# Six pairs of projection units by seven half products in a hybrid encoder layer

## The chip, the core and the metric

The kernel runs on one core of one Trainium2 chip. The core has five engines with a queue of instructions each: PE (TensorE, matmuls and the loads of their weights), DVE (VectorE), ACT (ScalarE), POOL (GpSimd) and SP, which here only issues DMA transfers. The metric is the device time of one execution in microseconds (us), lower is better.

## The reference, cut to what matters

One encoder layer on 512 tokens of width 1024: projections of `x`, partial rotary embedding, two attention mixers, sigmoid gates, an output projection, layer norm, a SwiGLU feed-forward part and a second layer norm.

```python
proj = h @ w_in[l]
qa, ka, va, qb, kb, vb = jnp.split(proj, SPLITS, axis=-1)
qa = rope_partial(qa.reshape(b, s, A_Q_HEADS, HEAD_DIM), pos)      
...
o_a = windowed_gqa_sink(qa, ka, va, a_sink[l])
o_b = dilated_mixture(qb, kb, vb)
gates = jax.nn.sigmoid(h @ w_gate[l] + b_gate[l])
g_a, g_b = jnp.split(gates, N_BRANCH, axis=-1)
mixed = g_a * (o_a @ w_br_a[l]) + g_b * (o_b @ w_br_b[l])
h = layer_norm(DN_ALPHA * h + mixed @ w_out[l], ln1_g[l], ln1_b[l])
f = (jax.nn.silu(h @ w_ff_gate[l]) * (h @ w_ff_up[l])) @ w_ff_down[l]
h = layer_norm(DN_ALPHA * h + f, ln2_g[l], ln2_b[l])
```

## The kernel before

Everything is float32 in and out, and matmuls run in fp32r. A float32 operand is therefore split into a high part (rounded to fp32r) and a low part (the rest), and each product is three matmuls: high times high, high times low, low times high. Making the two parts of a 128x512 tile is a copy (on ACT, or on DVE) and a subtraction on DVE.

Weights come in *units* of 128 output features by 1024 inputs. A unit is loaded as two halves of 128x512 (256 KB), each split by `half_unit` (line 389) into `h` and `l`. `feat_x` multiplies a unit with all of `x`: eight steps over the inputs, three matmuls of 512 columns each, 24 in all, into one PSUM bank. `xh` and `xl` are the two parts of `x`, features on the partitions and tokens along the columns.

What follows a unit depends on its kind. A query or key unit is rotated (`rotate`, line 514: a multiplication by cosines, a shuffle of partitions, a multiplication by sines and a sum, four DVE instructions on 128x512, although only 16 rows of each head's 64 rotate), split into parts, and moved by small DMAs into the layout that the scores want (`q_post`, `k_post`, `k_pairs`). A gate unit goes through a tanh (`gate`, line 1001) and waits in SBUF. A value unit is turned by transposes.

The string `ORDER` (line 79) lists the steps in program order: `q2` is a query unit of mixer A, `k1` a key unit, `g` a gate, `VA` the values, `A0` to `A3` the attention of mixer A by groups of heads, `Q`, `K`, `V` and `B` the same for mixer B. Behind it come the two branch products (L496 to L498 again), the output projection with the first layer norm (`tok_major`, L1192 to L1194) and the feed-forward part. There, pairs of gate and up units are already multiplied by *seven half products* (`quad` and its class, L1422 to L1424): a 2x2 block product of Winograd's form, whose factors are sums of quarter blocks and whose matmuls have 256 columns.

Order on the engines is set by `Program`: the code registers operations with their reads, writes and a priority, and a list scheduler in the kernel then emits them engine by engine, with planned durations and limits on buffers (`ws` staged weight halves, `whl` weight parts, `gen` other tiles). Weights have priority -130 us against the running sum of PE time, so they are fetched as early as their buffers allow: six staged halves and twelve parts while the projections run. Every engine then runs its list strictly in order. `load_sum` (line 367) loads one block and lets a DMA that accumulates, issued by POOL, add a second block to it; the feed-forward part uses it.

```python
def split(src, h, l, prio=0.0, abs_prio=None, hold=()):
    op(cp_alts(S), lambda e: copy(e, h.t, src.t), ...)                       # ACT or DVE
    op([(DVE, dve(S))], lambda e: nc.vector.tensor_tensor(l.t, src.t, f32(h.t), op=ALU.subtract), ...)
```

## Time and profile before

| | us |
|---|---|
| median of 3 runs | 737.44 (737.26 to 737.69) |
| the profiled execution, its own time | 737.0 |
| its span, first to last instruction | 735.2 |
| PE busy in the span | 725.2 |
| DVE busy | 653.7 |
| ACT busy | 447.4 |
| POOL busy | 109.5 |

The span is shorter than the execution's time by what lies around the program. A row of the profile's groups reads: line, engine, operation, tiles written <- tiles read (`ps` a PSUM bank, `sl` an SBUF tile, `x` the parts of `x`), shapes, count | busy time in us, mean ns of one | idle time of that engine just ahead of them and what ended it. Matmuls overlap, so the busy time of a group can be shorter than its count times its mean. A row of the timeline reads: start, length, engine, line, operation, tiles, count [idle ahead of it and what ended that]. A row of the windows gives the stretch, its length, and the busy time and count of PE, PEld (the loads of weights), DVE, ACT and POOL, the granted clock, the DMA engines' share and GB/s.

### The profile page before, as it was taken

What the parts mean: (1) busy time and instruction counts of PE and PEld (TensorE: products, weight loads), DVE (VectorE), ACT (ScalarE), POOL (GpSimd) and SP (SyncE); (2) the same over time, 40 slices, a digit from 0 to 9 for tenths busy, and PEclk for the clock granted to TensorE, in tenths of its full rate; (3) what the DMA queues carried; (4) which work ended last, traced back from release to release, by engine and by line L of the source; (5) the groups of instructions that cost most, each with busy time, mean ns of one, the idle gap of its engine ahead of it and who ended that gap; (6) DMA issues with size and microseconds to landing.
All of it is one profiled execution on the core that took longest, in us unless ns stands there. A gap on an engine that the chain in (4) does not pass through costs nothing.

```text
span 735.2 us, 13431 instructions
## 1 busy us (share of the span) xinstructions
PE 725.2 (99%) x4479; PEld 663.0 (90%) x4479; DVE 653.7 (89%) x1428; ACT 447.4 (61%) x1012; POOL 109.5 (15%) x273
## 2 busy tenths in 40 slices
PE   9999999999999999999999999999999999999995
PEld 6888888888888889888888999999999999999985
DVE  5879998898898999897686999799999999899977
ACT  5647687757665657774352567656666556666721
POOL 0000110000003323500010002111102111202100
PEclk9999999999999999999999999999999999999999
DMA  8824523437234765455583389776888978978402
GB/s 270 289 58 144 163 82 87 129 94 204 76 93 138 201 176 163 137 170 174 165 205 88 86 250 233 178 179 154 203 254 195 221 196 237 243 196 180 112 29 86
DMA packets 69252, 120.17 MB, mean 163 GB/s; under 512 B 8576, under 2 KB 12800, under 8 KB 69184
## 3 DMA queue, kind: packets, MB, share of 16 engines
q1 hardware_dynamic: 59040, 101.10, 44.7%
q0 software_dynamic: 9872, 18.09, 15.2%
q8 instruction: 35, 0.57, 0.3%
q14 instruction: 33, 0.27, 0.1%
q10 hardware_dynamic: 272, 0.13, 0.1%
HBM read 103.04 MB, written 2.10 MB: 143 GB/s over the span
## 4 chain that ended last, share of the span: by engine, by line
PE 94%; DMA 2%; DVE 2%; SPq 1%; ACT 1%; issue 0%; DVEq 0%; ACTq 0%
PE ps L497 12%; PE ps L496 12%; PE ps L498 12%; PE ps L1422 9%; PE ps L1424 9%; PE ps L1423 9%; PE ps L1633 4%; PE ps L1635 4%; PE ps L1634 4%; PE ps L749 3%; PE ps L1192 3%; PE ps L1193 3%; PE ps L1194 3%; PE ps L647 1%; PE ps L646 1%; PE ps L815 1%
## 5 line engine op out<-in xcount | busy, mean ns | idle before, releaser
L357 ACT ACTIVATE sl<-sl 128x512 fp32r<-128x512 f32 (+3 forms) x383 | 210.6, 582 | 62.0 <-DVE sl L1312 17.3
L1312 DVE TENSOR_TENSOR sl<-sl,sl 128x512 fp32r<-128x512 f32 (+3 forms) x294 | 167.1, 609 | 6.2 <-ACT sl L357 3.4
L357 ACT ACTIVATE sl<-ps 128x256 f32<-128x256 f32 (+5 forms) x205 | 85.8, 441 | 99.7 <-PE ps L1424 60.1
L496 PE MATMUL ps<-x,sl 128*128 128x512 f32 (+1 forms) x369 | 142.4, 386 | 0.3 <-ACT x L357 0.3
L498 PE MATMUL ps<-x,sl 128*128 128x512 f32 (+1 forms) x369 | 139.8, 379 | 0.0
L497 PE MATMUL ps<-x,sl 128*128 128x512 f32 (+1 forms) x337 | 127.9, 379 | 0.2 <-DVE x L469 0.2
L1422 PE MATMUL ps<-sl,sl 128*128 128x256 f32 x352 | 96.9, 275 | 0.6 <-ACT sl L357 0.6
L1423 PE MATMUL ps<-sl,sl 128*128 128x256 f32 x352 | 96.8, 275 | 0.0
L1424 PE MATMUL ps<-sl,sl 128*128 128x256 f32 x352 | 96.8, 275 | 0.0
L383 DVE TENSOR_TENSOR sl<-sl,sl 128x512 fp32r<-128x512 f32 x130 | 87.2, 685 | 5.1 <-ACT sl L357 4.5
L498 PEld LDWEIGHTS ps<-x,sl 128*128 128x128 f32 x369 | 69.9, 189 | 9.9 <-DVE sl L406 0.2
L496 PEld LDWEIGHTS ps<-x,sl 128*128 128x128 f32 x369 | 70.2, 190 | 8.7 <-ACT x L357 0.5
L371 POOL DMA_DIRECT2D sl<-wpack x44 | 38.5, 883 | 260.3 <-DMA sl<-wpack 72.7
L1422 PE MATMUL ps<-x,sl 128*128 128x256 f32 x264 | 72.6, 275 | 0.0
L1423 PE MATMUL ps<-x,sl 128*128 128x256 f32 x264 | 72.6, 275 | 0.0
L1424 PE MATMUL ps<-x,sl 128*128 128x256 f32 x264 | 72.6, 275 | 0.0
L497 PEld LDWEIGHTS ps<-x,sl 128*128 128x128 f32 x337 | 64.0, 190 | 7.5 <-DVE x L469 0.5
L1422 PEld LDWEIGHTS ps<-sl,sl 128*128 128x128 f32 x352 | 67.6, 192 | 0.8 <-ACT sl L357 0.7
L1423 PEld LDWEIGHTS ps<-sl,sl 128*128 128x128 f32 x352 | 67.6, 192 | 0.1
L1424 PEld LDWEIGHTS ps<-sl,sl 128*128 128x128 f32 x352 | 67.6, 192 | 0.0
L1422 PEld LDWEIGHTS ps<-x,sl 128*128 128x128 f32 x264 | 50.6, 192 | 0.4
L1423 PEld LDWEIGHTS ps<-x,sl 128*128 128x128 f32 x264 | 50.6, 192 | 0.4
(151 smaller groups left out, 1547.1 us busy)
## 6 DMA issues: line engine op xcount, KB each, us to landing
sl<-wpack SPq DMA_DIRECT2D x243, 256.0 KB, 3.7
sl<-sl SPq DMA_DIRECT2D x108, 128.0 KB, 2.3
wf<-wpack SPq DMA_DIRECT2D x51, 256.0 KB, 5.0
sl<-wpack POOLq DMA_DIRECT2D x44, 256.0 KB, 5.9
wf<-wpack POOLq DMA_DIRECT2D x24, 256.0 KB, 6.3
sl<-xtok SPq DMA_DIRECT2D x8, 256.0 KB, 3.3
out<-sl SPq DMA_DIRECT2D x7, 256.0 KB, 2.0
sl<-xT SPq DMA_DIRECT2D x6, 256.0 KB, 5.6
```

The lines of the kernel that those rows point to most:

```text
L357: nc.scalar.activation(dst, src, AF.Copy)
L371: op([(POOL, 1.0)], lambda e: nc.gpsimd.dma_start(b.t, src2, accum_op=ALU.add), reads=[b], writes=[b], prio=prio, moves=1.65)
L383: op([(DVE, dve(S))], lambda e: nc.vector.tensor_tensor(l.t, src.t, f32(h.t), op=ALU.subtract), reads=[src, h], writes=[l], prio=prio, abs ...
L496: mm(o, a, x0, start=(k == 0 and begins), stop=False, skip_group_check=split)
L497: mm(o, a, x1, start=False, stop=False, skip_group_check=split)
L498: mm(o, b, x0, start=False, stop=(k == nk - 1), skip_group_check=split)
L1312: op([(DVE, dve(w))], lambda e: nc.vector.tensor_tensor(dst(), x(), y(), op=o), reads=reads, writes=writes, prio=prio)
L1422: mm(o, wh, pairs(bh[k]()), start=(first and k == 0), stop=False, skip_group_check=True)
L1423: mm(o, wh, pairs(bl[k]()), start=False, stop=False, skip_group_check=True)
L1424: mm(o, wl, pairs(bh[k]()), start=False, stop=(k == 3), skip_group_check=True)
L1633: mm(ps.t, x0, pairs(w[0].t), start=(first and m == 0), stop=False, skip_group_check=True)
L1634: mm(ps.t, x0, pairs(w[1].t), start=False, stop=False, skip_group_check=True)
```

## The change

**Six pairs.** Twelve units of the first half of `ORDER` (q2 to q7, k1 and five gates) are taken in pairs `P:a,b` by `pair_x`, with the same seven half products as in the feed-forward part. A pair needs seven weight factors of 128x512 instead of four halves; two of them are sums made by an accumulating DMA, two are sums made on DVE, and all seven are split, the high part on ACT and the low part on DVE. Each of the seven products is 12 matmuls of 256 columns. Of `x`, three of the seven products take blocks as they are and four take combinations; `x_forms` makes the combinations once, in place in the tiles in which `x` was loaded, and splits them (16 DVE instructions on 128x256, 8 copies on ACT, 8 subtractions on DVE).

**Rotation.** At `R`, `turn_rows` gathers the 16 rotating rows of each head from two to four tiles into one tile by small DMAs, rotates that tile by the four DVE instructions, and sends the rows back by small DMAs. The tables of cosines and sines come once more in this layout, by 16 DMAs. Units outside the pairs are copied from PSUM on ACT first (`in_sbuf`). Nineteen units rotate so, in six steps `R`; the first three (k0, q0, q1) rotate as before.

**Low parts by DMA.** For the second half of each unit from Q00 to the output projection (two gates aside), `low_by_dma` writes `-w`, rounded, on ACT where the subtraction on DVE stood, and a DMA on POOL's queue adds `w` at full precision; the rounding of the negative copy leaves the same low part.

**Room.** `ws` is 8 and `whl` 16 until the last pair is done (`L`), then 6 and 12 as before; `gen` is 60. Five gates (of 8 to 15) are stored to DRAM behind their tanh and fetched again ahead of the branch products. `ORDER` is rewritten.

```diff
-N_WS, N_WHL, N_ATT = 6, 12, 16
+N_WS, N_WHL, N_ATT, N_GEN = 6, 12, 16, 60
 ORDER = """
-g2 VA q1 A0 q2 q3 A1 g k1 q4 g q5 A2 g q6 g q7 A3 g2
-Q00 K00 Q01 K01 V12 Q02 K02 V0 B0 Q10 K10 B1 Q11 K11 Q12 K12 B2 B3 g8
+X g2 VA q1 A0 P:q2,q3 P:k1,q4 R A1 P:g,g P:q5,g P:q6,q7 R A2 P:g,g A3 g2 L Q00 K00 Q01 K01 R V12 Q02 K02 R V0 B0 Q10 K10 Q11 K11 R B1 Q12 K12 R B2 B3 g7
 """
+BY_DMA = {*range(U_QKB, U_DOWN)} - {U_GATE + 8, U_GATE + 9}
+AWAY = range(8, 16)
+N_WSA, N_WHLA = 8, 16
...
     def half_unit(u, j):
         st, h, l = slot(F32, "ws"), slot(F32R, "whl"), slot(F32R, "whl")
         load(st, wpack[u, :, j * S:(j + 1) * S], prio=-LOOK)
+        if j == 1 and u in BY_DMA:
+            low_by_dma(st, h, l, wpack[u, :, j * S:(j + 1) * S], -LOOK)
+            return h, l
         split(st, h, l, prio=-LOOK, hold=[(l, "room")])
         return h, l
+    def low_by_dma(st, h, l, src, prio):
+        op(cp_alts(S), lambda e: copy(e, h.t, st.t), reads=[st], writes=[h, (l, "room")], prio=prio)
+        op([(ACT, act(S))], lambda e: nc.scalar.activation(l.t, st.t, AF.Copy, scale=-1.0), reads=[st], writes=[l], prio=prio)
+        op([(POOL, 1.0)], lambda e: nc.gpsimd.dma_start(l.t, src.bitcast(F32R), accum_op=ALU.add), reads=[l],
+           writes=[l], prio=prio, moves=1.65)
...
+    def x_forms():
...
+            tt(x11, x11, x12, ALU.subtract, a, a, HP, FORMS)
+            tt(x12, x22, x12, ALU.subtract, a + b, a, HP, FORMS)
+            minus_sum(x22, x11, x22)
+            minus_sum(x21, x22, x21)
+            for kk, toks in ((k, a), (k + 4, b)):
+                h, l = slot(F32R), slot(F32R)
+                parts((lambda h=h: h.t, h), (lambda l=l: l.t, l, (l, "room")), lambda b=xs[kk]: b.t, toks, S, FORMS)
+                XP[kk] = (h, l)
...
+    def pair_x(ua, ub):
...
+        for key in ("A11", "S1", "A12", "S3", "A22"):
+            fetch(key)
+        sep("A11")
+        sep("A12")
+        form("S2", "A11", "S1", "A11")
+        sep("S2")
+        sep("S1")
+        form("S4", "A12", "A12", "S2")
+        for key in ("S3", "S4", "A22"):
+            sep(key)
+        y, xz, t, v = bank("dense"), bank("dense"), slot(), slot()
+        def product(s, b, ps, tok, c, first, after=()):
...
+                for k in range(4):
+                    wh, wl = h.t[:, k * P:(k + 1) * P], l.t[:, k * P:(k + 1) * P]
+                    mm(o, wh, pairs(bh[k]()), start=(first and k == 0), stop=False, skip_group_check=True)
+                    mm(o, wh, pairs(bl[k]()), start=False, stop=False, skip_group_check=True)
+                    mm(o, wl, pairs(bh[k]()), start=False, stop=(k == 3), skip_group_check=True)
...
+        product("A11", "B11", y, "y", LO, True)
+        keep(t, LO, 1, y, "y", LO)
+        product("A12", "B21", xz, "x", LO, True)
+        product("S2", "T2", y, "y", LO, False)
+        keep(t, HI, 2, y, "y", LO)
+        product("S1", "T1", xz, "z", HI, True)
+        keep(v, HI, 2, xz, "z", HI)
+        product("S3", "T3", y, "y", LO, False)
+        product("S4", "B22", xz, "z", HI, False)
...
+        product("A22", "T4", y, "y", LO, False)
+        keep(v, LO, 1, y, "y", LO, -1.0)
...
+    def turn_rows(tiles):
...
+        for i, R in enumerate(tiles):
+            for h in range(2):
+                gs.append((G, 2 * i + h))
+                op([(SP, 0.1)], lambda e, R=R, i=i, h=h: nc.sync.dma_start(
+                    G.t[32 * i + 16 * h:32 * i + 16 * h + 16], R.t[64 * h:64 * h + 16]), reads=[(R, 1), (R, 2)], writes=[gs[-1]], prio=EV)
...
+    def put_away(f):
+        t, d = gz[f], Buf("dram", None, lambda: dram.tile([P, S], F32, name=name("gz")))
+        op([(SP, 0.73)], lambda e: nc.sync.dma_start(d.t, t.t), reads=[t], writes=[d], prio=EV)
```

Three places show how instructions stand now. The names are a tile and its number; `x` and `sl` are SBUF tiles.

On PE, early in mixer A, ahead of the first transposes of its probabilities. Before, the three matmuls of a step of unit q3, between them and the next step two matmuls of the scores (L646, L647):

```order
L496 MATMUL ps_610<-x_94,sl_443 128x512
L497 MATMUL ps_610<-x_103,sl_443 128x512
L498 MATMUL ps_610<-x_94,sl_444 128x512
L646 MATMUL ps_637<-sl_351,sl_599 128x256
L647 MATMUL ps_637<-sl_352,sl_599 128x256
L646 MATMUL ps_643<-sl_351,sl_599 128x384
```

Now, at the same row numbers, a product of the second pair with `x` as it is (`ps_705`), and behind it one of the first pair (`ps_620`), whose moving tiles are combinations of `x`:

```order
L627 MATMUL ps_705<-x_94,sl_610 128x256
L628 MATMUL ps_705<-x_103,sl_610 128x256
L629 MATMUL ps_705<-x_94,sl_611 128x256
L627 MATMUL ps_620<-sl_205,sl_506 128x256
L628 MATMUL ps_620<-sl_206,sl_506 128x256
L629 MATMUL ps_620<-sl_205,sl_507 128x256
```

Matmuls of 256 columns stand where matmuls of 512 stood, and products of two pairs alternate.

On DVE, while `x` arrives: before, only low parts of `x` (L469) and of the first weights (L406).

```order
L469 TENSOR_TENSOR x_103<-sl_131,x_94 128x512
L406 TENSOR_TENSOR sl_184<-sl_138,sl_183 128x512
L469 TENSOR_TENSOR x_204<-sl_147,x_192 128x512
L406 TENSOR_TENSOR sl_202<-sl_151,sl_201 128x512
L406 TENSOR_TENSOR sl_211<-sl_157,sl_210 128x512
L469 TENSOR_TENSOR x_204<-sl_164,x_192 128x512
L469 TENSOR_TENSOR x_204<-sl_168,x_192 128x512
L469 TENSOR_TENSOR x_204<-sl_175,x_192 128x512
```

Now the combinations (L532 with 256 columns, L558) and their low parts (L532 with 512) stand between them:

```order
L532 TENSOR_TENSOR sl_98<-sl_98 128x256
L484 TENSOR_TENSOR x_103<-sl_131,x_94 128x512
L532 TENSOR_TENSOR sl_73<-sl_147,sl_73 128x256
L420 TENSOR_TENSOR sl_187<-sl_138,sl_186 128x512
L484 TENSOR_TENSOR x_211<-sl_147,x_195 128x512
L532 TENSOR_TENSOR sl_206<-sl_73,sl_205 128x512
L420 TENSOR_TENSOR sl_215<-sl_152,sl_214 128x512
L420 TENSOR_TENSOR sl_223<-sl_159,sl_222 128x512
L484 TENSOR_TENSOR x_211<-sl_166,x_195 128x512
L484 TENSOR_TENSOR x_211<-sl_170,x_195 128x512
L484 TENSOR_TENSOR x_211<-sl_177,x_195 128x512
L558 SCALAR_TENSOR_TENSOR sl_147<-sl_73,sl_147 128x256
```

The first weights' low parts moved behind one or two of the new rows, and the rest of the combinations follows behind the last part of `x`.

On SP, at the first `R`: before, a query unit's four moves (L587) and then weights (L365).

```order
L587 DMA sl_752<-sl_734 64x512
L587 DMA sl_758<-sl_734 64x512
L587 DMA sl_752<-sl_735 64x512
L587 DMA sl_758<-sl_735 64x512
L365 DMA sl_788<-wpack 128x512
```

Now the gathers (L697) of the third and fourth tile, the weights (L369) between them, and the rows on their way back (L708):

```order
L697 DMA sl_819<-sl_749 16x512 x2
L369 DMA sl_999<-wpack 128x512
L697 DMA sl_819<-sl_915 16x512 x2
L369 DMA sl_1106<-wpack 128x512
L369 DMA sl_1109<-wpack 128x512
L369 DMA sl_1146<-wpack 128x512
L708 DMA sl_659<-sl_819 16x512 x2
L369 DMA sl_1170<-wpack 128x512
L708 DMA sl_724<-sl_819 16x512 x2
L369 DMA sl_1192<-wpack 128x512
L708 DMA sl_749<-sl_819 16x512 x2
L708 DMA sl_915<-sl_819 16x512 x2
```

Loads of weights that stood behind four moves now stand among gathers and returns, each of which can make the loads behind it wait.

More of the change, by code (lines that the diff above doesn't have):

```diff
@@ new lines, in parts, with hl, minus_sum @@
+    def parts(h, l, src, reads, n, prio, whole=True):
+        copy_by_act(h[0], src, n, False, reads, [h[1], l[2]], prio)
+        tt(l[0], src, lambda: f32(h[0]()), ALU.subtract, [*reads, h[1]], [l[1]], n, prio)
+    def hl(st, prio):
+        h, l = slot(F32R, "whl"), slot(F32R, "whl")
+        parts((lambda: h.t, h), (lambda: l.t, l, (l, "room")), lambda: st.t, [st], S, prio)
+        return h, l
+    XP, done_rows = {}, set()
+    def x_forms():
+        at = lambda k, n: (lambda b=xs[k]: b.t[:, n * HP:(n + 1) * HP])
+        key = lambda k: [(xs[k], 0), (xs[k], S // 2)] if k == 0 else [(xs[k], 0)]
+        for k in range(KD // 2):
+            a, b = key(k), key(k + 4)
+            x11, x12, x21, x22 = at(k, 0), at(k, 1), at(k + 4, 0), at(k + 4, 1)
+            def minus_sum(dst, x, y):
+                op([(DVE, dve(HP))], lambda e: nc.vector.scalar_tensor_tensor(
+                    dst(), x(), -1.0, y(), op0=ALU.mult, op1=ALU.subtract), reads=a + b, writes=b, prio=FORMS)
+            tt(x11, x11, x12, ALU.subtract, a, a, HP, FORMS)
[6 more added lines that the diff above has]
+                XP[kk] = (h, l)
@@ new lines, in x_tokens @@
+    def x_tokens(kind):
+        if kind[0] == "B":
+            j, n = int(kind[1]) - 1, int(kind[2]) - 1
+            ks = range(4 * j, 4 * j + 4)
+            mk = lambda m: [lambda k=k: m[k]()[:, n * HP:(n + 1) * HP] for k in ks]
+            return mk(xh), mk(xl), [t for k in ks for t in xtok_of(k)]
+        j, n = {"T1": (0, 0), "T3": (0, 1), "T4": (1, 0), "T2": (1, 1)}[kind]
+        v = [XP[k] for k in range(4 * j, 4 * j + 4)]
+        mk = lambda p: [lambda x=x: x[p].t[:, n * HP:(n + 1) * HP] for x in v]
+        return mk(0), mk(1), [b for x in v for b in x]
@@ L515, in rotate, with in_sbuf @@
+    def in_sbuf(u):
+        ps, t = bank("dense"), slot()
+        feat_x(ps, unit(u))
+        op([(ACT, act(S, True))], lambda e: copy(ACT, halves(t.t), back(ps.t)), reads=[ps], writes=[(t, 1), (t, 2)], prio=EV)
+        return t
     def rotate(ps):
+        if ps in done_rows:
+            return ps
+        if "slot" in ps.keys:
+            return turned(ps)
         R, Sh = slot(), slot()
@@ L671, in evac @@
                         copy(e, d, s)
[L673 removed]
+            op(cp_alts(S, True, 0.3 if turn_by else 0.1)[:2 if turn_by else 1], evac, reads=[ps], writes=[t], prio=EV if i else NORM)
             src.append(t)
```

155 lines of the change are left out of this document (132 added, 23 removed).

## The prediction

> **What bounds the kernel now.** I read the page first, then the windows by stage, then the timelines of PE and DVE. The page:
>
> ```profile
> span 735.2 us, 13431 instructions
> PE 725.2 (99%) x4479; PEld 663.0 (90%) x4479; DVE 653.7 (89%) x1428; ACT 447.4 (61%) x1012; POOL 109.5 (15%) x273
> PE 94%; DMA 2%; DVE 2%; SPq 1%; ACT 1%; issue 0%; DVEq 0%; ACTq 0%
> ```
>
> PE is busy throughout and the chain that ended last is PE's to 94%. A busy PE need not be a PE at its rate, since matmuls overlap. The timeline shows the rate by the distance of starts:
>
> ```profile
> 344.69 0.38 PE L496 MATMUL ps<-x,sl 128*128 128x512 f32 x1
> ...
> 346.63 0.38 PE L496 MATMUL ps<-sl,sl 128*128 128x512 f32 x1
> ...
> 444.77 0.28 PE L1423 MATMUL ps<-sl,sl 128*128 128x256 f32 x1
> ...
> 446.11 0.28 PE L1423 MATMUL ps<-sl,sl 128*128 128x256 f32 x1
> ```
>
> Nine starts lie between the first two rows, so a matmul of 512 columns costs 1.94/9 = 0.216 us; twelve between the other two, so one of 256 columns, in the half products of the feed-forward part, costs 1.34/12 = 0.112. The lengths, 0.38 and 0.28, are latency and must not be added up. By stage:
>
> ```profile
> 0.00:18.50 18.50, 16.81 (x68) 12.25 (x69) 10.86 (x25) 10.27 (x21) 0.90 (x5) 1.00 0.83 270
> 18.50:45.00 26.50, 26.50 (x130) 23.30 (x129) 19.39 (x37) 16.35 (x31) 1.66 (x8) 1.00 0.56 199
> 45.00:61.00 16.00, 16.00 (x80) 14.13 (x79) 15.96 (x41) 8.30 (x23) 2.36 (x7) 1.00 0.49 133
> 61.00:110.00 49.00, 49.00 (x269) 43.93 (x268) 44.81 (x115) 38.09 (x88) 5.05 (x17) 1.00 0.44 124
> 110.00:220.00 110.00, 110.00 (x587) 98.05 (x586) 101.56 (x265) 75.34 (x183) 6.48 (x34) 1.00 0.40 113
> 330.00:400.00 70.00, 69.57 (x324) 60.58 (x323) 50.44 (x82) 28.36 (x49) 6.05 (x7) 1.00 0.62 169
> ```
>
> From 18.5 us on PE never rests in the projections and the attention (26.50 of 26.50 to 110.00 of 110.00), at a granted clock of 1.00. So what the change takes off DVE gains nothing by itself there: only fewer columns through PE, or a wait put into PE, moves the end. But DVE is nearly full as well: 15.96 of 16.00 us from 45 to 61, 44.81 of 49.00 behind that. Its idle time lies at the start: 18.50 - 10.86 = 7.6 us in the first stretch and 26.50 - 19.39 = 7.1 us in the second.
>
> **What is removed from PE.** A pair was two units, 48 matmuls of 512 columns: 48 x 0.216 = 10.35 us. It becomes seven products of 12 matmuls of 256 columns: 84 x 0.112 = 9.38 us. Six pairs save 6 x 0.97 = 5.8 us. The rows of PE confirm it: 216 more in the order, six times 84 - 48, and all other shapes in equal number. That is the whole possible gain: 735.2 - 5.8 = 729.4 us of span.
>
> The Trainium skill speaks against it: its page "TensorE: Matmul & The Clock Gate", section "Back-to-back issue gap", gives 81 ns for a matmul of 128 columns and 131 ns for one of 512 in a sustained stream, because each also pays for its load of weights. An estimate on that page's line, 98 ns for 256 columns, would make a pair 84 x 0.098 - 48 x 0.131 = 1.9 us dearer, and the six 12 us. The spacings above, 0.216 and 0.112, contradict it in this kernel, so it keeps only a small chance below.
>
> **What is added to DVE, and when.** The first place where PE has to wait for DVE is the transposes of mixer A's first probabilities:
>
> ```profile
> 57.28 0.68 DVE L383 TENSOR_TENSOR sl<-sl,sl 128x512 fp32r<-128x512 f32 x1
> 57.88 0.01 DVE L519 LOAD_MASK_SELECT sl<-ps  x1
> 57.88 0.73 DVE L519 STREAM_SHUFFLE sl<-ps 128x512 f32<-128x512 f32 x1
> 58.51 0.16 DVE L805 RECIPROCAL st<-st 128x4 f32<-128x4 f32 x1
> 59.71 0.34 DVE L739 TENSOR_SCALAR sl<-sl,st 128x256 f32<-128x256 f32 x1
> ...
> 441.36 0.42 DVE L1312 TENSOR_TENSOR sl<-sl 128x256 f32<-128x256 f32 x1
> ...
> 442.70 0.68 DVE L1312 TENSOR_TENSOR sl<-sl,sl 128x512 fp32r<-128x512 f32 x1
> 61.05 1.04 PE L749 MATMUL ps<-ident,sl 128*128 128x128 f32 x8
> ```
>
> The row at 59.71 is DVE's last share in these probabilities and the PE row is the transposes, one microsecond later. The distances of starts are DVE's prices: 0.60 us for a 128x512 operation, 0.63 for a shuffle, and 1.34/4 = 0.34 for one on 128x256 (four lie between the two rows of 441 and 442). In the order, DVE has 95 rows up to that normalisation before, and 125 now: 17 more of 128x512 (low parts of seven factors a pair instead of four, sums of factors, parts of the combined `x`), 17 more of 128x256 (the combinations), two shuffles and two copies fewer. That is 17 x 0.60 + 17 x 0.34 - 2 x 0.63 - 0.6 = 14.0 us more ahead of the same point. PE now reaches this point 1.0 us later in its own work (so many columns more of projections stand ahead of it), at 62.0.
>
> DVE was busy 10.86 + 19.39 + 15.96 = 46.2 us up to 61.0. With 14.0 more it needs 60.2, so of the 14.8 us that it idled it may keep 1.8 if PE is not to wait. How much can it fill? These rows show the idle time:
>
> ```profile
> 3.78 0.42 DVE L469 TENSOR_TENSOR x<-sl,x 128x256 fp32r<-128x256 f32 x1 [2.64 <-ACT x L357]
> 8.51 0.69 DVE L469 TENSOR_TENSOR x<-sl,x 128x512 fp32r<-128x512 f32 x1 [1.00 <-ACT x L357]
> 12.02 0.69 DVE L469 TENSOR_TENSOR x<-sl,x 128x512 fp32r<-128x512 f32 x1 [0.77 <-ACT x L357]
> 14.05 1.37 DVE L406 TENSOR_TENSOR sl<-sl,sl 128x512 fp32r<-128x512 f32 x2
> 40.68 0.76 DVE L695 TENSOR_TENSOR sl<-ps,sl 128x256 fp32r<-128x256 f32 x2 [4.07 <-ACT sl L357]
> ```
>
> The 3.5 us before 3.78 stay, since no input has landed. The gaps at 8.51 and 12.02 can take the first three combinations (1.0 us), which the order puts there. The 4.07 us ahead of 40.68 vanish: combinations and weight factors are queued. Left are 3.5 us at the start, 0.6 more before 6 us, and of the 2.6 us in gaps from 8 to 12 us about 1.6: 5.7 us, where 1.8 are free. That makes a wait of 3.9. Against that, operations that waited for ACT one by one were spaced by 1.37/2 = 0.68 (their full length), and in a backlog go at 0.60; for some 30 of the 95 rows that gives back 2.4, a wait of 1.5. Between these ends I take 2.4.
>
> From there to about 110 us the six pairs run. In a pair DVE does 7 low parts, 2 sums of factors, one sum of two blocks (10 x 0.60) and 0.34, 6.3 us in 9.38 us of PE, with mixer A's softmax besides. Before, two query units cost it four low parts, eight operations of rotation and two low parts behind, 14 x 0.60 = 8.4 in 10.35. The rotations shrink from 22 times four operations to 9 times four, but the gate pairs had none. Softmax chains that left DVE 4.2 us idle in 61 to 110 will do so again, with less room; I put 0.6 us of wait there, between nothing and the 1.5 that a full repeat of the first wait's lower end would be. Behind 110 the removed rows leave DVE room, which PE cannot use.
>
> **Rotation in common.** Nineteen tiles each cost two gathers and two returns, 76 small DMAs, and 16 for the tables. The nearest rows:
>
> ```profile
> 54.56 2.39 SPq L587 DMA_DIRECT2D sl<-sl  x4
> sl<-sl SPq DMA_DIRECT2D x108, 128.0 KB, 2.3
> sl<-wpack SPq DMA_DIRECT2D x243, 256.0 KB, 3.7
> sl<-wpack POOLq DMA_DIRECT2D x44, 256.0 KB, 5.9
> ```
>
> At 0.60 us an issue (2.39/4) and 2.3 to land, a step of four tiles takes 8 x 0.60 + 2.3 out, 4 x 0.60 on DVE and 7.1 back, 16.6 us, then 2.6 us of parts and moves. The shortest cover in the order is at Q12 and K12: 125 matmuls, about 24 us of PE, between K12's last matmul and the first score that reads a tile of theirs, and that step has only two tiles (4.7 + 2.4 + 4.7 + 5 us). So it costs nothing; the rest have 30 us and more. What waits behind them on SP are loads of weights, late by a return at most, 7.1 us, against a room of six halves, 6 x 12 x 0.216 = 15.5 us. I take 0; without that cover it would be up to 5 us once.
>
> **Low parts by DMA.** 41 subtractions leave DVE (41 x 0.60 = 25 us, worth nothing on a PE without gaps), 41 copies go to ACT, which has room (75.34 of 110), and 41 loads to POOL's queue. A low part is ready after its load (3.7), two copies (0.62 each), POOL's 0.9 and 5.9 to land: 11.7 us, inside the 15.5. No term; with that cover gone, see the third rival. The accumulating loads cost DMA time:
>
> ```profile
> q1 hardware_dynamic: 59040, 101.10, 44.7%
> q0 software_dynamic: 9872, 18.09, 15.2%
> L371 POOL DMA_DIRECT2D sl<-wpack x44 | 38.5, 883 | 260.3 <-DMA sl<-wpack 72.7 <-DVE sl L1312 65.5 <-DVE sl L1148 51.9
> ```
>
> q1 moves 256 KB (0.262 MB) in 0.447 x 735.2 x 0.262/101.1 = 0.85 us of all engines, q0 in 1.62. Five gates stored and fetched add ten of the former.
>
> **The sum.** Span 735.2 - 5.8 + 2.4 + 0.6 = 732.4. The profiled execution's own time is 737.0, 1.8 above its span, and the median 737.44, 0.44 above that: **734.6 us**.
>
> **Rivals.**
>
> *All hidden* (0.15): DVE's early work fits because loads land sooner or fewer waits bind, and PE never waits. 737.4 - 5.8 = 731.6. For it: PE rests nowhere from 18.5 to 220 us in the windows above, with the same dense DVE. Against it: 14.0 us more DVE work into 14.8 us of idle time, 4.1 of it before 6 us.
>
> *DVE becomes the bound of the first 110 us, and the kernel slower* (0.12). Its queue is in order: if the combinations of `x` stand ahead of rows whose inputs are there already, or themselves wait for late tiles, the gaps are not filled but shifted. If all 14.8 us of idle time stayed, the normalisation would come 14.0 us later, at 59.7 + 14.0 + 0.3 = 74.0 instead of 62.0, a wait of 12.0: 737.4 - 5.8 + 12.0 = 743.6. The point where it decides: slower than before once DVE idles more than 1.8 + 5.8 = 7.6 us ahead of the first transposes.
>
> *The DMA engines* (0.13). From 330 to 400 us they were busy 0.62 x 70 = 43 us. Some 15 accumulating loads belong there now (15 x 1.62 = 24) and five fetched gates (4.3): 72 us of 70. The surplus of 2.3, with loads landing late behind it, would make PE wait about 3 us beside DVE's: 737.6. For it: a landing of 5.9 us as median already. Against it: weights are fetched ahead, and with 0.83 of share in the first 18.5 us transfers still came.
>
> *The change does not do what it says* (0.03): a 256-column matmul costs more than half of a 512 one where moving tiles come from many SBUF tiles. With the lengths instead of the spacings, six times 84 x 0.28 - 48 x 0.38 = 32 us more, 769; the page's estimate above would give 749. The quads of the feed-forward part already run so at 0.112.
>
> **How the numbers follow.** The forecast has 0.57. Its own range is 732.5 to 736.3 (waits of 1 to 4.7). The range of eight in ten reaches down to the case without a wait and up into the DMA rival and the first part of the DVE rival, 731.6 to 738.8. What three runs can tell from no change is about 0.2%, 1.5 us: faster means below 736.0, slower above 738.9. Faster: 0.53 of the forecast, all 0.15 of *all hidden*, 0.02 of the DMA case, 0.70. Same: 0.04 + 0.09 + 0.04 (DVE half filled), 0.17. Slower: 0.08 + 0.02 + 0.03, 0.13.
>
> **What would show it.** PE's windows of 20 us between 45 and 110 should show starts of 256-column matmuls 0.112 apart and rows of PE with idle time ahead, ended by DVE or by ACT behind DVE, of 3 us in sum, most of them between 45 and 65 us. DVE should have no gap of 4 us before its first value parts, and still a few behind 110. The stretch from 110 to the branch products should be without waits on PE, as before. If PE's waits there are longer than 1 us and end on a DMA, rotation or low parts are priced wrongly; if they sit between 330 and 400 and end on weights, the DMA rival holds; if the early waits exceed 5.8 us, DVE was the bound and the kernel is not faster.

## The result and the profile after

The changed kernel is slower: 761.54 us median of six runs (759.33 to 765.28) against 737.72 for the kernel before on the same chip, a ratio of 1.033 (95% interval 1.030 to 1.036). The profiled execution took 763.23 us, its span is 761.5; the span before was 735.2. So 26.3 us came on top where 2.8 were forecast to go.

The page of the changed kernel:

```profile
span 761.5 us, 14271 instructions
PE 730.9 (96%) x4695; PEld 671.7 (88%) x4695; DVE 645.9 (85%) x1419; ACT 481.0 (63%) x1084; POOL 149.7 (20%) x326
PE 82%; DVE 5%; DMA 2%; ACT 2%; issue 1%; SPq 1%; DVEq 0%; ACTq 0%
...
sl<-sl SPq DMA_DIRECT2D x108, 128.0 KB, 3.5
```

The chain that ended last was PE's to 94% and is so to 82%. DVE is busy for 85% of the span where it was for 89%, ACT for 63% where it was for 61%: no engine has become the bound, waits have come in. The same stages as in the prediction, of the changed kernel (length, then busy time of PE, PEld, DVE, ACT and POOL, PE's granted clock, DMA share, GB/s):

```profile
18.50:45.00 26.50, 23.72 (x110) 20.48 (x109) 22.80 (x46) 16.60 (x30) 3.46 (x4) 0.96 0.89 261
45.00:61.00 16.00, 14.98 (x112) 13.99 (x110) 15.97 (x37) 10.92 (x26) 4.56 (x10) 0.96 0.57 105
61.00:110.00 49.00, 44.03 (x369) 43.30 (x370) 42.33 (x92) 34.79 (x83) 7.14 (x14) 0.98 0.78 201
110.00:220.00 110.00, 106.95 (x596) 95.39 (x596) 90.51 (x243) 78.62 (x190) 15.52 (x50) 0.95 0.62 157
220.00:330.00 110.00, 102.32 (x554) 91.28 (x554) 77.82 (x231) 72.91 (x185) 31.21 (x103) 0.97 0.69 166
330.00:400.00 70.00, 70.00 (x361) 62.17 (x360) 54.57 (x126) 47.73 (x105) 28.66 (x74) 1.00 0.95 255
```

PE rested nowhere from 18.5 to 330 us before (from 220 to 330, which the prediction does not show, it was busy for 110.00 of 110.00). Now it rests 2.8, 1.0, 5.0, 3.0 and 7.7 us in the first five of these stages, 19.5 in sum, and in the same stages its clock is under 1.00: 0.04 x 26.5 + 0.04 x 16 + 0.02 x 49 + 0.05 x 110 + 0.03 x 110 = 11.5 us at most, since part of the low clock falls into the waits. With the 5.8 us that PE has less to do, 26.3 + 5.8 = 32.1 us are to be explained; waits and clock are up to 31.0 of them. What PE waited for (us in total, times, longest):

```profile
PE ps L1153 <- DVE sl L983: 7.7, 1, 7.7
PE ps L627 <- ACT sl L635: 4.4, 2, 4.0
PE ps L890 <- ACT sl L361: 2.8, 1, 2.8
PE ps L1024 <- ACT sl L361: 2.3, 1, 2.3
PE ps L855 <- DMA sl<-sl: 1.6, 1, 1.6
```

A few long waits, at 312.7, 108.5, 43.4, 214.5 and 62.0 us. The longest, in the chain of waits of the changed kernel (start, length, what; the issues of L841 are eight):

```profile
300.07 0.34 PE ps L958 x3
300.48 1.18 SPq L841
...
305.17 0.58 SPq L841
305.80 0.59 SPq L697
306.43 1.94 DMA sl<-sl
...
308.48 0.09 DVE sl L700
...
312.23 0.35 DVE sl L983
312.71 1.20 PE ps L1153 x4
```

and on SP and DVE at the same time:

```profile
296.01 3.77 SPq L796 DMA_DIRECT2D sl<-sl  x6
299.88 5.87 SPq L841 DMA_DIRECT2D sl<-sl  x8
305.80 1.23 SPq L697 DMA_DIRECT2D sl<-sl  x2
308.46 0.01 DVE L700 LOAD_MASK_SELECT sl<-sl  x1 [7.98 <-DMA sl<-sl]
```

Read it from the end. PE wants the low part (L983) of a tile of probabilities. PE's transposes for that tile (L958) ended at 300.4, but L983 stands in DVE's queue behind a common rotation's shuffle (L700), which waited 7.98 us for rows. The last two gathers of rows (L697) were issued at 305.8, because moves (L796 and L841) of the *previous* common rotation's tiles stood ahead of them in SP's queue, the fourteen shown at 0.63 to 0.73 us each (3.77/6, 5.87/8) and ten more before them: 24 in all, from 287.5 to 305.75 us. The tile that these gathers read had been copied out of PSUM by 284.1.

At 108.5 and 214.5 it is the same queue with another victim, ScalarE:

```profile
98.61 7.72 SPq L796 DMA_DIRECT2D sl<-sl  x10
106.01 0.63 ACT L361 ACTIVATE sl<-sl 128x512 fp32r<-128x512 f32 x1 [4.35 <-DMA sl<-sl]
203.10 5.04 SPq L841 DMA_DIRECT2D sl<-sl  x8
208.24 4.89 SPq L369 DMA_DIRECT2D sl<-wpack  x8
213.19 0.63 ACT L361 ACTIVATE sl<-sl 128x512 fp32r<-128x512 f32 x1 [5.09 <-DMA sl<-wpack]
```

In the first, ScalarE's copy (L361) waits 4.35 us until one of these ten moves has landed: the move was issued at 100.92 and landed at 105.58, 4.66 us later (the median of all moves is 3.5), at a DMA share of 0.91 in these 20 us. So there the bunch is late by its landing as well as by its issue. In the second there are eight moves, and the weight loads begin at 208.24, so that a copy of weights holds ScalarE for 5.09 us, with what PE needs behind it.

That reading made the theories for the experiments. *SP*: SyncE's queue, filled by the common rotation's gathers, returns and collected moves, is late, and DVE and ACT stand in order. *DMA*: the accumulating loads fill the DMA engines, and transfers land late. *VectorE*: the pairs overload DVE.

### The profile page after: what moved, and what is told of

It is laid out like the page before. It is cut to its first block, busy times and chain, and to the rows that moved or that the text cites. A ratio compares the mean times of both kernels' runs of the same rounds, so it can differ in the third digit from the quotient of the medians.

```text
span 761.5 us, 14271 instructions
## 1 busy us (share of the span) xinstructions
PE 730.9 (96%) x4695; PEld 671.7 (88%) x4695; DVE 645.9 (85%) x1419; ACT 481.0 (63%) x1084; POOL 149.7 (20%) x326
## 4 chain that ended last, share of the span: by engine, by line
PE 82%; DVE 5%; DMA 2%; ACT 2%; issue 1%; SPq 1%; DVEq 0%; ACTq 0%
PE ps L1658 9%; PE ps L1659 9%; PE ps L1660 9%; PE ps L511 7%; PE ps L512 7%; PE ps L513 7%; PE ps L1869 4%; PE ps L1871 4%; PE ps L1870 4%; PE ps L958 3%; PE ps L1448 2%; PE ps L1450 2%; PE ps L1449 2%; DVE sl L532 2%; PE ps L627 2%; PE ps L629 2%
## 5 line engine op out<-in xcount | busy, mean ns | idle before, releaser
L361 ACT ACTIVATE sl<-sl 128x512 fp32r<-128x512 f32 (+3 forms) x404 | 224.0, 584 | 66.9 <-DVE sl L532 25.4
L532 DVE TENSOR_TENSOR sl<-sl,sl 128x512 fp32r<-128x512 f32 (+3 forms) x360 | 209.5, 620 | 9.3 <-ACT sl L635 4.3
L361 ACT ACTIVATE sl<-ps 128x256 f32<-128x256 f32 (+6 forms) x208 | 88.7, 442 | 98.5 <-PE ps L1660 55.6
L511 PE MATMUL ps<-x,sl 128*128 128x512 f32 (+1 forms) x273 | 107.6, 394 | 0.6 <-ACT x L361 0.6
L375 POOL DMA_DIRECT2D sl<-wpack x56 | 49.0, 890 | 285.7 <-DMA sl<-wpack 106.6
L513 PE MATMUL ps<-x,sl 128*128 128x512 f32 (+1 forms) x273 | 104.5, 383 | 0.0
L512 PE MATMUL ps<-x,sl 128*128 128x512 f32 (+1 forms) x241 | 93.0, 386 | 0.3 <-DVE x L484 0.2
L405 POOL DMA_DIRECT2D sl<-wpack x41 | 35.4, 864 | 181.9 <-ACT sl L404 74.5
L513 PEld LDWEIGHTS ps<-x,sl 128*128 128x128 f32 x273 | 52.6, 193 | 7.8 <-DVE sl L420 0.2
L511 PEld LDWEIGHTS ps<-x,sl 128*128 128x128 f32 x273 | 53.0, 194 | 7.2 <-ACT x L361 1.3
L512 PEld LDWEIGHTS ps<-x,sl 128*128 128x128 f32 x241 | 46.7, 194 | 6.0 <-DVE x L484 1.1
L1659 PEld LDWEIGHTS ps<-x,sl 128*128 128x128 f32 x264 | 50.6, 192 | 0.4
L1658 PEld LDWEIGHTS ps<-x,sl 128*128 128x128 f32 x264 | 50.6, 192 | 0.4
```

The lines of the kernel that those rows point to most:

```text
L361: nc.scalar.activation(dst, src, AF.Copy)
L375: op([(POOL, 1.0)], lambda e: nc.gpsimd.dma_start(b.t, src2, accum_op=ALU.add), reads=[b], writes=[b], prio=prio, moves=1.65)
L405: op([(POOL, 1.0)], lambda e: nc.gpsimd.dma_start(l.t, src.bitcast(F32R), accum_op=ALU.add), reads=[l], writes=[l], prio=prio, moves=1.65)
L511: mm(o, a, x0, start=(k == 0 and begins), stop=False, skip_group_check=split)
L512: mm(o, a, x1, start=False, stop=False, skip_group_check=split)
L513: mm(o, b, x0, start=False, stop=(k == nk - 1), skip_group_check=split)
```

## The experiments

All are edits of the changed kernel. Times are medians; ratios are to the kernel before on the same chip, with their 95% intervals.

**No low parts by DMA.**

```diff
-BY_DMA = {*range(U_QKB, U_DOWN)} - {U_GATE + 8, U_GATE + 9}
+BY_DMA = set()
```

> Pairs and common rotation stay; every low part is a subtraction on VectorE again, so 41 accumulating loads of 256 KB are gone. Theory DMA: the waits go with the traffic, 735 to 745. Theory SP: gathers, returns and moves are as many and as bunched, so the waits stay in number and place, 754 to 765. Theory VectorE: 25 us more on VectorE, slower than 761.5.

760.36 us, 1.031 (1.028 to 1.033). 41 accumulating loads fewer, and 1.2 us gained; waits of 5.0 and 4.8 us stay. So these loads were not the cause, as the SP theory has it; that VectorE has its subtractions back in this kernel is in the number too.

**No pairs.** `P:` steps make two units (`T:` for a query or key, a gate put away for a gate); no combined forms of the input, and the smaller limits on staged weights (6 and 12) from the start.

```diff
         if w == "X":
-            x_forms()
+            pass
...
-            both = [units_of(x) for x in w[2:].split(",")]
+            for x in w[2:].split(","):
+                if x == "g":
+                    step("G")
+                else:
+                    step("T:" + x)
+            return
...
```

> The pairs are undone: two units each, with 48 matmuls of 512 columns; common rotation and low parts by DMA stay, and all gates of the pairs are still put away. Theory SP: the long waits stay, at R, and the 5.8 us of TensorE come back: 755 to 768. Theory DMA: the pairs' 18 additional loads are gone, 745 to 760. Theory VectorE: the first 110 us run as before, 737 to 745.

754.32 us, 1.023 (1.020 to 1.025): just under the SP theory's range and inside the DMA theory's. What PE waited for, without pairs:

```profile
PE ps L1086 <- DMA sl<-sl: 4.3, 1, 4.3
PE ps L855 <- DMA sl<-sl: 2.2, 2, 1.3
PE ps L1024 <- ACT sl L361: 1.6, 1, 1.6
```

Long waits remain, the two largest on moved tiles, and the one at 43 us (L890) is gone. So the kernel is slower without the pairs too, and the pairs make a wait of their own. This run still has the low parts by DMA and the gates put away; that the rotation is what counts in it rests on the run before and on the three gate pairs below, which keep both and lose almost nothing.

**Every tile turned for itself**, by the four VectorE operations; six fewer general slots, since with 60 the planner finds no order for this kernel.

```diff
-            turn_rows(tiles)
-            done_rows.update(tiles)
...
-N_WS, N_WHL, N_ATT, N_GEN = 6, 12, 16, 60
+N_WS, N_WHL, N_ATT, N_GEN = 6, 12, 16, 54
```

> Every tile is turned for itself on VectorE (four operations of 128x512), so the 76 gathers and returns of rows and the 16 table loads are gone; pairs, low parts by DMA and the place of the moves stay; six fewer general slots (54 for 60), since each tile needs one more while it is turned. Theory SP (SyncE's one queue issues gathers, returns and a bunch of moves behind them at 0.6 us each, and VectorE and ScalarE stand in order behind rows that wait for them): the 7.8 us wait near 312 us, whose chain runs through the gathers, is gone with its slow clock, and part of the others: 738 to 750. Theory VectorE: VectorE gets 19 x 4 operations for 7 x 4, 48 x 0.6 = 29 us more, and is the bound: 762 or more. Should neither hold and only the bunch of moves count, it stays near 758.

758.5 us, 1.029 (1.027 to 1.031): outside both theories, and at the number named for the bunch of moves alone, but it cannot be read that way. The wait on L983 fell from 7.7 to 3.0 us, as the SP theory has it, but DVE now has its old work and the pairs' (672.8 us busy for 645.9), and new waits came between 80 and 100 us: the longest there, 2.8 us, ends on ScalarE (L946), a second, 1.3 us, on DVE (L1007). With the low parts on DVE as well:

> Only the six pairs, the gates put away and the collected moves stay: each tile turned for itself, every low part on VectorE; 54 general slots. Theory SP: about the time of the kernel with each tile turned for itself, less 0 to 3 us or more, 736 to 750. Theory VectorE: 29 + 25 us more on VectorE than after the change, waits in the first 110 us: 750 to 770.

777.15 us, 1.053 (1.052 to 1.055). So giving up either alone costs nothing (758.5 and 760.36 for 761.54), and giving up both costs 15.6 us: together they relieve VectorE by what the pairs need, as the VectorE theory has it. Waits come in either way, so this pair of runs cannot tell SP's share.

**The rows by another queue**, all else in place and order.

```diff
-                op([(SP, 0.1)], lambda e, R=R, i=i, h=h: nc.sync.dma_start(
+                op([(SP, 0.1)], lambda e, R=R, i=i, h=h: nc.gpsimd.dma_start(
```

in both places, gathers and returns.

> The order on every engine is that of the changed kernel; only the 76 transfers of rows (gathers and returns) are issued from GpSimd's queue instead of SyncE's, at the same places of the order. Theory SP: SyncE has 76 x 0.6 = 46 us less to issue, the gathers do not stand behind eight moves and the weights do not stand behind returns: the wait of 7.8 us near 312 us shrinks by the 5 us of moves ahead of the gather, the others by 1 to 2 each, 745 to 756. Theory that the latency of the round trip itself counts, wherever it is issued: no change or slower by the longer landing from that queue (5.9 for 2.8 us), 760 to 770.

753.81 us, 1.021 (1.020 to 1.023): 7.7 us gained with the same work in the same order, by 76 issues fewer on SP. PE is busy for 20.00 of 20.00 us from 200 to 220, and its wait for L983 fell from 7.7 to 1.1 us. **The moves by that queue** instead:

```diff
-        op([(SP, 0.4)], lambda e: nc.sync.dma_start(f32(dst.t[d:d + 64]), f32(src.t[c:c + 64])), reads=[src],
+        op([(SP, 0.4)], lambda e: nc.gpsimd.dma_start(f32(dst.t[d:d + 64]), f32(src.t[c:c + 64])), reads=[src],
```

and the same in `k_pairs`.

> The order on every engine is that of the changed kernel; only the moves of half tiles (the 108 of 128 KB) are issued from GpSimd's queue instead of SyncE's. Theory SP, with the bunch of moves as its worst part: weights and gathers come 4 to 7 us earlier at 100, 205 and 300 us, the waits there shrink: 742 to 755. Theory DMA (the engines are full, 0.91 of them from 100 to 120 us, and any queue only shares them): no change, 758 to 765; GpSimd's own issue cost of about 0.9 us each for 108 of them could make it slower.

766.82 us, 1.039 (1.037 to 1.042), slower: outside the ranges of both theories. These moves now land after 6.2 us (median) where they took 3.5, and what slowed them (GpSimd's issues, or the accumulating loads that now stand behind the moves in its queue) was not taken apart. It does not decide between SP and DMA; the next run does.

**Each move in two halves**: the same bytes, 108 issues more.

```diff
-        op([(SP, 0.4)], lambda e: nc.sync.dma_start(f32(dst.t[d:d + 64]), f32(src.t[c:c + 64])), reads=[src],
+        op([(SP, 0.4)], lambda e: [nc.sync.dma_start(f32(dst.t[d + i:d + i + 32]), f32(src.t[c + i:c + i + 32])) for i in (0, 32)], reads=[src],
```

> The order on every engine is that of the changed kernel; each move of 64 partitions is issued as two of 32 at the same place of SyncE's queue: the same bytes, twice the issues. If SyncE's issue of the moves sets the waits: a bunch of 8 takes up to 8 x 0.6 = 5 us more, at some six bunches, 775 to 800. If the bytes on the DMA engines set them: within 4 us of 761.5.

805.53 us, 1.093 (1.090 to 1.095), 44.0 us more than the changed kernel. The same place as above, in SP's timeline, the DMA queue during it (packets, MB, share of 16 engines), and PE's longest wait:

```profile
324.45 8.32 SPq L796 DMA_DIRECT2D sl<-sl  x13
332.88 10.03 SPq L841 DMA_DIRECT2D sl<-sl  x16
342.95 1.23 SPq L697 DMA_DIRECT2D sl<-sl  x2
```

```profile
q1 hardware_dynamic: 1421, 1.93, 40.7%
```

```profile
PE ps L1153 <- DVE sl L983: 22.0, 1, 22.0
```

29 issues of 64 KB take 18.35 us, 0.63 each, as long as those of 128 KB did (3.77/6), and the wait behind them grows from 7.7 to 22.0 us while this queue keeps the DMA engines busy to 41% and POOL's adds 8%. Here the number of issues sets the waits, not the bytes. In the changed kernel the two queues kept the DMA engines busy to 74% and 25% while its 24 moves were issued (287 to 306 us), and some of those issues took more than 1 us; whether full engines lengthen an issue was not taken apart.

**The planner's prices.** The order is a list plan in which every DMA of SP's queue holds it for 0.47 us. Only these prices change:

```diff
-                        end = now + 0.47
+                        end = now + {0.1: 0.6, 0.4: 0.75}.get(cost, 0.47)
...
-                        o.done = moved + 0.87
+                        o.done = moved + (0.87 if now < 20 else 1.87)
```

> Only three prices in the planner change: SyncE is held 0.60 us by a row transfer and 0.75 by a move instead of 0.47, and a transfer of SyncE's queue lands 1.0 us later than the planner had it; the same work, in an order that allows for them. Theory SP (the order was made for a queue that issues faster than the traced one, so in-order engines meet waits that the plan did not have): most of the waits behind 80 us go, those of the pairs at 43 stay, 740 to 750. Theory that the transfers are too many whatever the order: 755 to 765.

758.79 us, 1.029 (1.027 to 1.032); with the rows in GpSimd's queue too, in plan and program:

> As the kernel with the planner's three prices changed, and the gathers and returns of rows are GpSimd's in the plan and in the program. Theory SP: the better of the two measures together, 738 to 748. Theory that GpSimd's landings of about 6 us a step, twice in a rotation, are worse than SyncE's queue once the plan allows for it: 748 to 760.

749.7 us, 1.017 (1.015 to 1.019). These two orders give an output other than the reference's, for a reason that is not known; the same 4695 matmuls run in them, so they tell where PE waits, but they are no kernels to use. In the first of them PE was busy for 40.00 of 40.00 us from 60 to 100 and 20.00 of 20.00 from 200 to 220 and from 300 to 320; but the wait at 43 us grew from 2.8 to 5.9, and from 320 to 440 PE rested 8.2 us where it had rested 0.8. So the theory's places were right and its total was not: both times lie in the range of the other theory. A second set of prices, with the loads of the rotation's tables later:

```diff
+                        late = 20 < now < 340
+                        end = now + ({0.1: 0.6, 0.4: 0.75}.get(cost, 0.5) if late else 0.47)
+                        moved = max(moved, now + 0.9) + (1.5 if now < 5 else 1.1 if late else 0.92) * cost
+                        o.done = moved + (0.87 + 1.0 if late else 0.87)
...
-                       writes=[(b, i)], prio=-130)
+                       writes=[(b, i)], prio=-60)
```

> The planner's prices from 20 to 340 us of its own time are nearer to the trace (SyncE held 0.60 us by a row transfer, 0.75 by a move, 0.50 by a load; a transfer of SyncE's queue and an accumulating one land 1.0 us later; 1.10 for 0.92 in the DMA engines' share), and the 16 loads of the rotation's tables are asked for 70 us later. Theory SP: no wait over 1 us between 60 and 320 us; and if the 3.95 us for which VectorE stands near 33 us come from table loads ahead of a weight load, the wait at 43 us falls from 6.1 us to under 3: 742 to 750. If that wait is VectorE's backlog from the pairs alone, it stays at 3 to 6 us: 748 to 757.

748.0 us, 1.015 (1.013 to 1.018), and with the rows in GpSimd's queue

> As the kernel with the planner's prices and the later tables, and the gathers and returns of rows go by GpSimd's queue, in the plan and the program. Theory SP: the least of all, 736 to 744. If the wait at 43 us is VectorE's backlog from the pairs alone: 742 to 750.

746.87 us, 1.014 (1.012 to 1.017): above the SP theory's 744. In both the wait at 43 us is gone, which answers the question that the first of them asked: the row of DVE that stood for an accumulated sum of weights there, 2.71 us in the changed kernel and 3.78 with the first set of prices, stands 1.39 us in the first of these two. The pairs' early work still costs about as much: PE rests 2.9 us from 40 to 60 us there, for 3.2 in the changed kernel, now at products of the pairs, with DVE busy for 19.90 of 20.00. The three worst stretches of the changed kernel in windows of 20 us, and two of the same with the new prices and the old queue:

```profile
100.00:120.00 20.00, 16.02 (x115) 15.75 (x114) 12.44 (x32) 13.30 (x34) 2.31 (x6) 0.83 0.91 250
200.00:220.00 20.00, 17.18 (x75) 13.96 (x74) 13.79 (x40) 10.87 (x28) 2.94 (x10) 0.84 0.88 220
300.00:320.00 20.00, 12.32 (x57) 10.66 (x56) 10.01 (x23) 6.37 (x13) 1.73 (x3) 0.83 0.79 204
```

```profile
100.00:120.00 20.00, 19.72 (x158) 18.61 (x156) 17.15 (x42) 15.42 (x36) 3.33 (x8) 1.00 0.97 270
300.00:320.00 20.00, 20.00 (x103) 17.72 (x102) 10.62 (x29) 12.13 (x28) 3.18 (x7) 1.00 1.06 276
```

The transfers and their queues are the same, some ten copies changed from DVE to ACT, and PE is busy for 20.00 of 20.00 us where it rested for 7.68, at a DMA share of 1.06 as the profile counts it. So the DMA engines could carry it; the order had not allowed for the time that SP's queue takes. A part comes back later: from 330 to 370 us, where the changed kernel had no wait, PE rests 3.8 us in the kernel with the second set of prices and the rows in GpSimd's queue.

**R behind every two tiles**, so bunches of half the size.

> R stands behind every two tiles instead of every three or four: the same 76 row transfers and as many moves, in bunches of half the size, and 4 x 4 to 5 x 4 more VectorE operations of up to 0.6 us. If the size of a bunch sets the waits: 742 to 754. If the number of transfers sets them: 758 to 768.

766.72 us, 1.040 (1.037 to 1.042): smaller bunches gained nothing, as the theory of the number has it. The kernel also has more VectorE rows, so this alone does not show that the number counts.

**Three pairs of gates, the old rotation.** Gates need no rotation; queries and keys are single units turned out of PSUM, as before the change.

```diff
-X g2 VA q1 A0 P:q2,q3 P:k1,q4 R A1 P:g,g P:q5,g P:q6,q7 R A2 P:g,g A3 g2 L Q00 K00 Q01 K01 R V12 Q02 K02 R V0 B0 Q10 K10 Q11 K11 R B1 Q12 K12 R B2 B3 g7
+g2 VA q1 A0 X q2 q3 A1 g k1 q4 P:g,g q5 A2 q6 P:g,g q7 P:g,g A3 g2 L Q00 K00 Q01 K01 V12 Q02 K02 V0 B0 Q10 K10 B1 Q11 K11 Q12 K12 B2 B3 g5
...
-N_WS, N_WHL, N_ATT, N_GEN = 6, 12, 16, 60
+N_WS, N_WHL, N_ATT, N_GEN = 6, 12, 16, 49
...
```

> Three pairs of gate tiles stay, the query and key tiles are single units and are rotated out of PSUM as before the change, so no row transfers, no collected moves; low parts by DMA stay; 49 general slots as before the change. TensorE has 3 x 0.97 = 2.9 us less than before. Theory SP (the losses of the change are those of the common rotation's transfers): 734.5 to 738. Theory that pairs cost their saving again by VectorE and accumulating weight sums: 738 to 745.

738.86 us, 1.002 (1.001 to 1.003), as the second theory has it: the 2.9 us saved were lost again, and the waits in the profile are of 1.1 us at most. With every low part on VectorE:

> As the three gate pairs, with every low part on VectorE. If the accumulating loads cost nothing and VectorE's room is what counts: slower than with them, 736 to 745. If they cost by the DMA engines' time: faster than with them by 1 us or more.

742.63 us, 1.007 (1.006 to 1.009): the accumulating loads save 3.8 us here. The same three pairs behind A2, with the combined forms asked for behind q3, planned with the second set of prices, and with the old prices:

> The three gate pairs stand behind A1 and later instead of from k1 on, the combined forms of the input are made behind the first query units, and the planner has the traced prices of the transfers. If early VectorE work of the pairs made waits in the first 60 us: those are gone, 734 to 737. Otherwise the same as the kernel with three gate pairs and low parts by DMA, within 2 us.

> Three late gate pairs with the old rotation and the planner's old prices. If the place of the pairs decides: 737 to 738.5, as with the traced prices. If the prices decide: 738.5 to 742.

737.82 us, 1.0005 (0.9996 to 1.0014), and 737.5 us, 1.0008 (0.9995 to 1.0022): the prices make no difference here, and both are even with the kernel before. The later place may be worth the 1.4 us between 738.86 and 737.5, but the intervals of the two overlap. By the first theory the waits of the first 60 us should have gone, and they did not: the one at the value tiles is 1.1 and 1.0 us, where it was 0.6 at the early place. Last, the same three late pairs with the combined forms of the input held back behind mixer A's value tiles (and the second prices only up to 300 us):

```diff
...
+            for o in pr.ops[n0:]:
+                env["held"].succ.append(o)
+                o.left += 1
```

> Three late gate pairs, traced prices (up to 300 us), and every operation on the combined forms of the input depends on the last operation of mixer A's value tiles. If the forms, ahead of those tiles' copies in the in-order queues, made the wait near 42 us: it is gone there (under 0.3 us), and some 14 us of VectorE work move behind it, where VectorE is full: waits of 3 to 7 us between 75 and 110 us, 738 to 744. If the wait has another cause: it stays at 1 us or more.

739.31 us, 1.003 (1.002 to 1.004). Its windows:

```profile
40.00:60.00 20.00, 20.00 (x101) 17.52 (x100) 17.85 (x38) 8.48 (x16) 2.45 (x3) 1.00 0.56 109
60.00:100.00 40.00, 38.30 (x213) 34.46 (x211) 39.29 (x94) 27.15 (x61) 4.28 (x15) 1.00 0.66 165
```

The wait of 1.1 us at the value tiles is gone (20.00 of 20.00), and one of 2.5 us comes at 100.8, behind a stretch in which DVE is full, 39.29 of 40.00. In these three late pairs it was the forms. For the changed kernel's wait at 43 us this does not show it; its own rows, below, name an accumulated sum of weights. No version that was run is faster than the kernel before.

## Why the prediction was wrong

**PE's rate and the saving: right.** Pairs of the changed kernel run at the price that was used; ten starts lie between these rows, 0.111 us each:

```profile
56.82 0.28 PE L628 MATMUL ps<-sl,sl 128*128 128x256 f32 x1
...
57.93 0.28 PE L629 MATMUL ps<-sl,sl 128*128 128x256 f32 x1
```

**VectorE's early work: that PE would wait was right, the place and the cause were not, and the size was too small.** The forecast had 2.4 us (1.5 to 3.9) at 62 us, behind mixer A's probabilities. The main wait came at 43.4, 2.8 us, at the value tiles' transposes (L890):

```profile
37.20 0.69 DVE L532 TENSOR_TENSOR sl<-sl,sl 128x512 f32<-128x512 f32 x1 [2.71 <-DMA sl<-wpack]
37.26 1.94 ACT L361 ACTIVATE sl<-sl 128x512 fp32r<-128x512 f32 x3 [2.50 <-DMA sl<-wpack]
40.39 2.46 ACT L361 ACTIVATE sl<-sl 64x512 fp32r<-64x512 f32 x4 [0.62 <-DVE sl L732]
42.75 0.64 ACT L361 ACTIVATE sl<-ps 128x256 f32<-128x256 f32 x2
```

DVE stood 2.71 us and ScalarE 2.50 for the same accumulated sum of weights, which POOL had issued at 29.85 and which landed at 37.18. PE had nothing more to do for the values from 40.7, but ScalarE had four late copies to make first, the first of them for the end of a rotation on DVE (L732), and copied the values out of PSUM (the last row) from 42.75 on. The idle time of 4.07 us ahead of the value parts was not there to be filled at no cost: the rows that were to fill it wait for transfers themselves, and stand in front of rows that PE needs. With 0.4 us at 56.6 and 1.6 at 62.0 the early waits are 4.8 us, where 3.0 were forecast for all of them. The one at 62.0 (L855) is for a tile of q1, which rotates as before the change; its last move was issued at 58.51, behind a load of weights. (DVE's additional work in the prediction adds up to 14.1 us and not 14.0, which changes nothing.)

**The failed step: "Rotation in common", "So it costs nothing".** It took the way of one step's tiles, 16.6 us, and set it against the distance to the first score that reads them. That cover held in the changed kernel, where no score waits for a tile that was rotated in common (the first gather is issued at 62.1, after the score that waited at 62.0). It is not a safe one: with the rows in GpSimd's queue a score waits 2.8 us for its moved tile (L1086). Three things were missing.

First, the moves. They were counted as 2.6 us of "parts and moves", but a group of Q10, K10, Q11 and K11 releases 4 + 8 + 4 + 8 = 24 moves at once, 24 x 0.63 = 15 us of SP's queue, and 18.3 us in the trace. Before, four or eight moves came with each unit. The moves, not the returns, are what gathers, a copy and weights waited for; "late by a return at most, 7.1 us" is one bunch too few.

Second, who waits. The cover was that of the tile's own reader. The one that waits first is DVE or ACT, which run in order, and every row behind the shuffle or the copy waits with it: PE's 7.7 us were for a tile that has nothing to do with rotation.

Third, no work behind it hides it. DVE had gained room behind 110 us (90.51 of 110.00), but room is of no use to an engine that stands.

**Low parts by DMA: 0 was close**, 760.36 without them for 761.54; with three gate pairs and the old rotation they gain 3.8 us.

**The rivals.** The DMA rival put its wait between 330 and 400 us; PE was busy for 70.00 of 70.00 there at a DMA share of 0.95. The VectorE rival's mechanism, rows of the pairs that wait for late tiles ahead of rows that are ready, is the wait at 43 us, at 2.8 us instead of 12.0; the late tile was a sum of weights and not a combination of `x`. The sign of the result came from a step priced at zero and under no rival of its own: the "up to 5 us once" was three waits, 7.7, 4.0 and 2.3 us, 14.0 in sum, and the clock behind them. The text did name a sign to look for, waits over 1 us behind 110 us that end on a DMA; PE's waits there end on DVE and ACT, and it is these that stood at a DMA.

## What to carry to other kernels

When vector work is replaced by small DMAs, price the queue that issues them: count every issue of the step and of the steps that it releases together, at the traced time of one issue and not by bytes. Then look for the first in-order engine that stands at a transfer, and ask what else is queued behind that row; the cover of the moved tile's own reader is not enough. A list plan is only as good as the price of its cheapest-looking resource: nearer prices, with the rotation's tables loaded later, gave back 13.5 of the 23.8 us lost.

## What was not expected of the hardware

An issue on SyncE's queue takes about the same for 64 KB (0.63 us) as for 128 KB (5.87/8 = 0.73 with its waits) and for 32 KB (1.23/2 = 0.61): here it goes by the count.

PE's clock falls during a wait, and stays down behind it. Windows of the changed kernel from the wait at 312.7:

```profile
307.00:309.00 2.00, 0.00 (x0) 0.00 (x0) 0.54 (x2) 0.98 (x2) 0.86 (x1) 1.00 0.43 135
309.00:311.00 2.00, 0.00 (x0) 0.00 (x0) 2.00 (x6) 0.00 (x0) 0.00 (x0) 0.51 0.99 230
314.00:316.00 2.00, 2.00 (x8) 1.73 (x8) 1.78 (x4) 1.11 (x2) 0.00 (x0) 0.53 0.19 41
316.00:318.00 2.00, 2.00 (x11) 1.75 (x10) 1.30 (x5) 1.18 (x3) 0.00 (x0) 1.00 0.68 226
```

The last matmul before it ended at 305.0; the clock is 1.00 to 309, 0.51 behind, and 1.00 again from 316, 3.3 us after PE went on. Behind the wait at 108.5 it stayed at 0.50 until 114. At that clock matmuls of 512 columns start 0.43 us apart for 0.22, so half of the time is lost, and these waits cost 1.5 to 3 us more than their length; the wait of 1.6 us at 62.0 left the clock at 1.00. The Trainium skill, page "TensorE: Matmul & The Clock Gate", section "Part 1: The HAM clock gate (the "warmup" mystery)", has the array fall to half rate after an idle window of about 3.4 us. The trace agrees on the half rate, and on the delay only roughly: 4.0 us here, but 2.1 at the wait of 43.4, where the clock is 0.50 from 42.8 on and PE had gone on to 40.7. The prediction had priced its waits without it.
